# Last x rows loaded ahead, list rows of the last tiles scattered later, first expert's tokens and weights made ready ahead of a loop

## The chip, the cores and the metric

The kernel runs on one core of one Trainium2 chip. The metric is the device time of one execution in microseconds (us); the median of three executions is taken. Engines are named as in the profile: PE (TensorE matmuls) with PEld (its weight loads), DVE (VectorE), ACT (ScalarE), POOL (GpSimd), SP (SyncE). A q behind the name (SPq, POOLq) is the engine's sequencer, where DMA issues, branches and semaphore waits are recorded.

## What is computed

One decoder layer over 4096 tokens of width 1024: a normed and modulated input, a sliding-window attention beside a gated recurrence, an output projection, a residual, and then a mixture of 32 experts in 4 groups, of which each token takes two.

```python
h = rmsnorm(x, ln1_pre) * (1 + sc1) + sh1
attn, hg = ...                                # attention, recurrence
mix = concat([attn, hg]) @ w_out
x = x + ga1 * rmsnorm(mix, ln1_post)          # x rows are read again here
h = rmsnorm(x, ln2_pre) * (1 + sc2) + sh2
g = top1(softmax(h @ w_rg + b_rg))            # group of the token
e = top2(softmax(logits of that group))       # its two experts, weights normed
y = sum over the two: w_e * ((silu(h @ w_gate[e]) * (h @ w_up[e])) @ w_down[e])
x = x + ga2 * rmsnorm(y, ln2_post)
```

## The kernel before

The tokens are 32 tiles of 128 rows. Every float32 product is made of three products of split parts. Stage one (`sweep1`) makes the projections of the recurrence, stage two (`sweep2`) attention, output projection, residual, second norm and routing, stage three (`experts`) the experts. A planner (`Weave`) writes out the order: generators yield what they wait for, a model clock (`Clock`) holds a due time for each, and the instruction of whichever is due is recorded next. What results is one fixed order for each engine, and each engine runs its own in order.

Names for the end of stage two, tile n:

- `g_out(n)`: output projection into PSUM `ps_j`, two halves of 512 columns; ACT sums the squares and DVE multiplies by `mod0`, both into `ym`, shown as tile `x` (three buffers, so `ym` of tile 31 takes that of tile 28).
- `g_post(n)`: loads the x rows of the tile (`xt`, shown as `xr`, two buffers) by a DMA on SP; POOL makes the root (`ryv`, `ryr`); DVE makes the residual `x<-x,ryr,xr`; SP writes it to `out`. DVE or POOL makes `h2` in the same tile `xr`; its root is `r2v`, `r2r`. SP writes `h2` to `h_d`. Tiles up to 29 then turn `h2` with a DMA transpose on SP (`h2T<-x`), tiles 30 and 31 on PE (`ps_t<-ident,xr`). PE makes the logits (`ps_s<-wr,h2T`), DVE adds the bias (`s<-ps_s,rs,br`).
- `g_route(m)`: for a batch of tiles (m=6: tiles 24 to 27; m=7: 28 and 29; m=8: 30 and 31) some forty small DVE operations find the two experts, the place in each expert's queue, and add to the running counts `cum`. Then POOL issues three scatters for each tile, each behind a small memset: two rows of `tab_d` (token, row of y, weight; one for each expert) and one row of `list_d` (token number by its row in the group).
- `g_order`: between these, the experts in order of their size (`eord`), from the counts after tile 27.

Stage three. Expert r in that order is place r; it has room for a fixed number of tokens (`CAPS`, up to 384, so two or three tiles). SP loads the three matrices of place 0 (`ws`) as soon as `eord` is there. A loop whose count `n_over` is only known on the chip (lines 1986 and 1987) does what exceeds the room; here the count is zero, and it is jumped over. Behind it POOL gathers `trow`, the table rows of all places, PE turns them, DVE makes `tok` (token numbers), `yrow` and `wgt`; POOL gathers the token rows of place 0 (`xg<-h_d,tok`, four buffers). For each place PE turns the tokens (`ps_x`), ACT and DVE split them (`xT`), PE makes gate and up (`ps_g`), then down (`ps_d`); ACT and DVE split the weights (`w<-ws`, eight buffers). POOL scatters the results to `y_d`. `g_list` works out the rows of the list and reads the list back (`ti`), for the last step, which adds both results of a token, norms them and adds them to `out`.

Of the kernel before, what the change touches and what calls it, by code (L numbers as in the profile page):

```python
# [214 lines left out]
class Ring:  # L215
# [10 lines left out]
    def next(self):  # L226
        return self.slots[len(self.out) % self.bufs]
# [45 lines left out]
class Layer:  # L273
# [59 lines left out]
    def setup(self, ctx):  # L333
# [21 lines left out]
        self.pm = cst.tile([32, 32], F32, name="pm")  # L355
        self.cap = cst.tile([P, 32], BF, name="cap")
        self.trows = cst.tile([P, 1], I32, name="trows")
        self.spacer = cst.tile([1, 1], F32, name="spacer")

    def pools(self, ctx):  # L360
# [780 lines left out]
    def sweep2(self, w16a):  # L1141
# [7 lines left out]
        with ExitStack() as ctx:  # L1149
# [207 lines left out]
            def g_out(n):  # L1357
                while ("mT", n) not in st or (n >= 3 and ("h2T", n - 3) not in st):
                    yield WAIT
                mT = st["mT", n]  # L1360
                yield [mT]
                ym = xp.tile([P, D], F32, name="x", bufs=3)
                ss = sm.tile([P, 2], F32, name="ssy")
                for c in range(2):
                    pj = ps_j.tile([P, 512], F32, name="ps_j")
                    for k in range(KC):
                        while ("wo", k) not in st:
                            yield WAIT
                        for i, (u, v) in enumerate(((0, 0), (0, 1), (1, 0))):
                            nc.tensor.matmul(pj, mT[:, k, v], wo[:, k, u, c * 512:(c + 1) * 512],  # L1370
                                             start=(k == 0 and i == 0), stop=(k == KC - 1 and i == 2))
                        yield 0
                    yc = ym[:, c * 512:(c + 1) * 512]
                    nc.scalar.activation(yc, pj, AF.Square, scale=osc[:, 3:4], accum_out=ss[:, c:c + 1])
                    nc.vector.tensor_tensor(yc, pj, G1[:, c * 512:(c + 1) * 512], op=ALU.mult)
                st["y", n] = ym, ss
                wv.add(g_post(n))

            def g_post(n):
# [2 lines left out]
                while "fill" not in st:  # L1382
                    yield WAIT
                ym, ss = st["y", n]
                xt = op.tile([P, D], F32, name="xr")
                nc.sync.dma_start(xt, a["x"][0, n * P:(n + 1) * P, :])
                yield [ss, ym]
                r = self.rstd(sm, ss[:, 0:1], 1, D, "ry", also=ss[:, 1:2])
                yield
# [79 lines left out]
            def g_route(m):  # L1469
# [118 lines left out]
                yield  # L1588
                nc.vector.tensor_mul(pl[:, :, 1, 2], pl[:, :, 0, 2], gm[:, 3])
                nc.vector.tensor_add(cum, cum, cs)  # L1590
                if m == max(0, NT // RB - 2):
                    wv.add(g_order())
                st["routed", m] = True
# [3 lines left out]
                for b in range(B):  # L1597
                    for c in range(2):
                        self.scatter(self.tab_d, sl[:, c, b:b + 1], pl[:, b, c], "tab", "other rows of the table")
                        yield rest  # L1600
                    self.scatter(self.list_d, sl[:, 2, b:b + 1], idi[:, n0 + b:n0 + b + 1], "list",
                                 "other rows of the list")
                    yield rest
# [238 lines left out]
    def experts(self):  # L1842
# [5 lines left out]
        with ExitStack() as ctx:  # L1848
# [122 lines left out]
                return nc.sync.value_load(eord[0:1, r:r + 1], min_val=0, max_val=31)  # L1971

            order = ((0, 0), (1, 0), (0, 1), (1, 1), (2, 0), (2, 1))
            places = [(r, i, f) for r in range(32) for i, f in order]


            st, lows = {}, []
# [3 lines left out]
            rp = ent(tc.tile_pool(name="r_p", bufs=1, reuse_waits="tile"))  # L1981
            steps = self.order(cp, rp, ps_x)
            next(steps)


            n_over = nc.values_load(self.nover[0:1, 0:1], min_val=0, max_val=P)
            with tc.For_i(0, n_over, 1) as it:
# [36 lines left out]
                    out=self.y_d, out_offset=bass.IndirectOffsetOnAxis(ap=oi[:, 2:3], axis=0), in_=y,  # L2024
                    in_offset=None, bounds_check=2 * T - 1, oob_is_err=False)
                for ring in (W, XG, XT, Y, YY):
                    ring.gone.update(ring.out)


            for _ in range(2):  # L2030
                next(steps)
            for j in range(tile_n[0]):
                load_x(0, j, run(XG.take()))
            run(steps)

            eord = cp.tile([P, 32], I32, name="eord")
            nc.gpsimd.tensor_copy(eord, self.eord)
# [124 lines left out]

            def g_list():

                yield 12000.0
                yield from self.list_rows(cp, fp)
                yield
                y = yield from Y.take()
# [114 lines left out]
```

## Time and profile before

| | us |
|---|---|
| median of three executions | 2732.44 (2731.12 to 2740.7) |
| profiled execution, its own time | 2765.53 |
| span of the profile | 2763.8 |
| PE busy in the span | 2510.2 (91%) |
| DVE busy | 1905.7 (69%) |
| ACT busy | 1360.1 (49%) |
| POOL busy | 756.7 (27%) |

The page's row of busy tenths for PE is 9 nearly throughout, with a hole at about two thirds of the span, where stage two ends and stage three begins, and another in the last 50 us. The granted clock is full elsewhere, with short falls, and half in these two holes.

### The profile page before, as it was taken

To read this page: it belongs to the slowest core of one execution; us is meant where nothing else is said; L and a number is where in the kernel's file an instruction comes from. 1 tells how busy PE (TensorE), PEld (TensorE's weight loads), DVE (VectorE), ACT (ScalarE), POOL (GpSimd) and SP (SyncE) were. 2 spreads that over 40 slices of the span, in tenths; PEclk is the share of its full clock that TensorE was granted. 3 is DMA by queue.
4 is the path that set the end of the run, shared out by engine and by line. 5 is a ranking of instruction groups with operands and counts; after the bars stand their busy time and mean duration, and the time that the engine had idled before them with its cause. 6 is when DMAs were issued, how large, how long until landed. Compare 5 with 4: busy or idle time off the path is not lost. (4 is left out here: it accounts for less than half of the span.)

```text
span 2763.8 us, 50275 instructions
## 1 busy us (share of the span) xinstructions
PE 2510.2 (91%) x19433; PEld 1916.5 (69%) x19433; DVE 1905.7 (69%) x4109; ACT 1360.1 (49%) x2935; POOL 756.7 (27%) x1069
## 2 busy tenths in 40 slices
PE   5989999999999999989999999955999999999992
PEld 2767677677667676666666676624888888889981
DVE  5657657777776688878778778664555666566774
ACT  4435444334333355555555545523545656666662
POOL 0111212211211012132232331343442333233336
PEclk9999999999999999999999999977999999999996
DMA  8212222222222334343453453445655878788987
GB/s 278 88 62 77 96 72 73 83 91 75 70 88 83 109 119 126 119 93 97 117 117 93 108 115 94 77 129 187 215 174 188 295 258 270 280 274 286 324 284 215
DMA packets 194619, 414.46 MB, mean 150 GB/s; under 512 B 89069, under 2 KB 124057, under 8 KB 172873
## 3 DMA queue, kind: packets, MB, share of 16 engines
q1 hardware_dynamic: 157216, 319.06, 36.6%
q0 software_dynamic: 31584, 91.58, 11.3%
q8 instruction: 153, 2.51, 0.4%
q10 hardware_dynamic: 5576, 0.58, 0.2%
q14 instruction: 90, 0.73, 0.1%
HBM read 284.60 MB, written 118.16 MB: 146 GB/s over the span
## 5 line engine op out<-in xcount | busy, mean ns | idle before, releaser
L140 PE MATMUL ps_g<-xT,w 128*128 128x256 f32 (+8 forms) x3072 | 461.5, 305 | 0.0
L140 PEld LDWEIGHTS ps_g<-xT,w 128*128 128x128 f32 x3072 | 436.2, 189 | 7.1 <-issue 0.3
L140 PE MATMUL ps_j<-w,mT 128*128 128x512 f16 x1536 | 368.2, 384 | 0.0
L140 PE MATMUL ps_j<-hT,w 128*128 128x256 f16 x3072 | 349.0, 274 | 4.9 <-POOL hT L140 4.9
L140 PE MATMUL ps_j<-w,hT 128*128 128x512 f16 x1536 | 349.7, 380 | 0.0
L140 PEld LDWEIGHTS <-w 128*128 128x128 f16 x3072 | 301.9, 98 | 47.1 <-issue 8.4
L140 PEld LDWEIGHTS <-hT 128*128 128x128 f16 x2304 | 196.6, 99 | 167.2 <-issue 6.7
L140 PE MATMUL ps_d<-w,av 128*128 128x512 f32 (+6 forms) x1020 | 269.1, 407 | 3.9 <-ACT av L140 3.5
L140 ACT ACTIVATE w<-ws 128x512 fp32r<-128x512 f32 (+1 forms) x392 | 246.1, 678 | 32.5 <-issue 23.5
L140 DVE TENSOR_TENSOR w<-ws,w 128x512 fp32r<-128x512 f32 x384 | 245.3, 685 | 5.4 <-ACT w L140 5.3
L140 PEld LDWEIGHTS <-mT 128*128 128x128 f16 x1536 | 144.3, 99 | 148.4 <-issue 12.3
L140 DVE TENSOR_TENSOR xT<-ps_x,xT 128x256 fp32r<-128x256 f32 (+8 forms) x256 | 115.5, 472 | 170.3 <-ACT xT L140 160.2
L140 PE MATMUL ps_j<-hT,w16a 128*128 128x256 f16 x1920 | 222.4, 275 | 0.0
L140 PEld LDWEIGHTS ps_d<-w,av 128*128 128x128 f32 (+6 forms) x1020 | 177.6, 182 | 51.6 <-ACT av L140 5.2
L140 PEld LDWEIGHTS <-w16a 128*128 128x128 f16 x1920 | 188.1, 99 | 25.7 <-issue 0.6
L140 POOL TENSOR_TENSOR hT<-hf,hT 128x512 f16<-128x512 f32 x64 | 103.6, 1619 | 270.0 <-ACT hT L140 255.2
L140 ACT ACTIVATE y<-ps_d,wgt 128x512 f32<-128x512 f32 (+4 forms) x144 | 99.0, 688 | 121.2 <-PE ps_d L140 88.5
L140 PE MATMUL ps_x<-ident,xg 128*128 128x128 f32 (+7 forms) x680 | 127.4, 294 | 28.5 <-DMA xg<-h_d,tok 23.9
L140 ACT ACTIVATE s<-s,mx,qsc 128x256 f32<-128x256 f32 (+1 forms) x256 | 148.8, 584 | 0.0
L140 PEld LDWEIGHTS ps_x<-ident,xg 128*128 128x128 f32 (+7 forms) x680 | 106.3, 193 | 56.5 <-DMA xg<-h_d,tok 28.3
L140 ACT ACTIVATE xT<-ps_x 128x256 fp32r<-128x256 f32 (+8 forms) x256 | 101.3, 422 | 88.5 <-PE ps_x L140 80.2
L140 POOL DMA_INDIRECT y_d<-y,yrow x85 | 91.1, 1072 | 193.3 <-ACT y L140 153.9
(397 smaller groups left out, 4242.3 us busy)
## 6 DMA issues: line engine op xcount, KB each, us to landing
ws<-in_w_exp_gate_dram SPq DMA_DIRECT2D x32, 1024.0 KB
ws<-in_w_exp_up_dram SPq DMA_DIRECT2D x32, 1024.0 KB
ws<-in_w_exp_down_dram SPq DMA_DIRECT2D x32, 1024.0 KB
yy<-y_d SPq DMA_DIRECT2D x24, 1024.0 KB
x<-in_x_dram SPq DMA_DIRECT2D x32, 512.0 KB
hT_d<-hT SPq DMA_DIRECT2D x16, 1024.0 KB
m_w<-in_w_ada_dram SPq DMA_DIRECT2D x128, 128.0 KB
hT<-hT_d SPq DMA_DIRECT2D x16, 1024.0 KB
```

What stands on the lines that cost most here:

```text
L140: r = f(*a, **kw)
```

## The change

Three things. (1) At tile 30's output projection the x rows of tiles 30 and 31 are loaded into one buffer that held a block of stage one's `hT` (shown as tile `hT`), and `g_post` of these two tiles uses it instead of `xr`; no load is issued there. (2) The list rows of tiles 24 to 31 are not scattered by `g_route`; DVE keeps a copy of their places (`lsl`), and `g_list` scatters the eight columns in stage three, 3000 ns of planner's time apart, ahead of its other work. (3) Ahead of the loop over `n_over` stand now the gather of `trow`, its transposes, `tok`, the gathers of place 0's tokens, and the split of its gate and up weights. The loop's own buffers are counted so that what is held stays held.

```diff
--- before.py
+++ after.py
@@ -355,6 +355,7 @@
         self.pm = cst.tile([32, 32], F32, name="pm")
         self.cap = cst.tile([P, 32], BF, name="cap")
         self.trows = cst.tile([P, 1], I32, name="trows")
+        self.lsl = cst.tile([P, 8], I32, name="lsl")
         self.spacer = cst.tile([1, 1], F32, name="spacer")
 
     def pools(self, ctx):
@@ -1358,6 +1359,12 @@
                 while ("mT", n) not in st or (n >= 3 and ("h2T", n - 3) not in st):
                     yield WAIT
                 mT = st["mT", n]
+                if n >= NT - 2:
+                    if n == NT - 2:
+                        st["lx"] = Cut(hp.tile([P, KC, 2, NB], F16, name="hT", bufs=2))
+                        for i in (n, n + 1):
+                            st["lx", i] = st["lx"].tile([P, D], F32)
+                            nc.sync.dma_start(st["lx", i], a["x"][0, i * P:(i + 1) * P, :])
                 yield [mT]
                 ym = xp.tile([P, D], F32, name="x", bufs=3)
                 ss = sm.tile([P, 2], F32, name="ssy")
@@ -1382,8 +1389,11 @@
                 while "fill" not in st:
                     yield WAIT
                 ym, ss = st["y", n]
-                xt = op.tile([P, D], F32, name="xr")
-                nc.sync.dma_start(xt, a["x"][0, n * P:(n + 1) * P, :])
+                if n >= NT - 2:
+                    xt = st["lx", n]
+                else:
+                    xt = op.tile([P, D], F32, name="xr")
+                    nc.sync.dma_start(xt, a["x"][0, n * P:(n + 1) * P, :])
                 yield [ss, ym]
                 r = self.rstd(sm, ss[:, 0:1], 1, D, "ry", also=ss[:, 1:2])
                 yield
@@ -1588,6 +1598,9 @@
                 yield
                 nc.vector.tensor_mul(pl[:, :, 1, 2], pl[:, :, 0, 2], gm[:, 3])
                 nc.vector.tensor_add(cum, cum, cs)
+                if n0 >= NT - 8:
+
+                    nc.vector.tensor_copy(self.lsl[:, n0 - NT + 8:n0 - NT + 8 + B], sl[:, 2])
                 if m == max(0, NT // RB - 2):
                     wv.add(g_order())
                 st["routed", m] = True
@@ -1598,6 +1611,8 @@
                     for c in range(2):
                         self.scatter(self.tab_d, sl[:, c, b:b + 1], pl[:, b, c], "tab", "other rows of the table")
                         yield rest
+                    if n0 >= NT - 8:
+                        continue
                     self.scatter(self.list_d, sl[:, 2, b:b + 1], idi[:, n0 + b:n0 + b + 1], "list",
                                  "other rows of the list")
                     yield rest
@@ -1971,7 +1986,7 @@
                 return nc.sync.value_load(eord[0:1, r:r + 1], min_val=0, max_val=31)
 
             order = ((0, 0), (1, 0), (0, 1), (1, 1), (2, 0), (2, 1))
-            places = [(r, i, f) for r in range(32) for i, f in order]
+            places = [(r, i, f) for r in range(32) for i, f in order][4:]
 
 
             st, lows = {}, []
@@ -1981,6 +1996,29 @@
             rp = ent(tc.tile_pool(name="r_p", bufs=1, reuse_waits="tile"))
             steps = self.order(cp, rp, ps_x)
             next(steps)
+            next(steps)
+
+            def first_weights(fs):
+
+                for i, f in fs:
+                    ws = st["ws", 0, i]
+                    w = run(W.take())
+                    t, part = pieces(w, ws, i, f)
+                    for p in part:
+                        nc.scalar.activation(p[0], p[2], AF.Copy)
+                        low(*p)
+                    st["w", 0, i, f] = t, w
+                    if f:
+                        WS.drop(ws)
+
+
+            first_weights(order[:2])
+            next(steps)
+            for j in range(tile_n[0]):
+                load_x(0, j, run(XG.take()))
+            run(steps)
+            first_weights(order[2:4])
+            held = {R: len(R.out) for R in (W, XG, XT, Y, YY)}
 
 
             n_over = nc.values_load(self.nover[0:1, 0:1], min_val=0, max_val=P)
@@ -2024,14 +2062,8 @@
                     out=self.y_d, out_offset=bass.IndirectOffsetOnAxis(ap=oi[:, 2:3], axis=0), in_=y,
                     in_offset=None, bounds_check=2 * T - 1, oob_is_err=False)
                 for ring in (W, XG, XT, Y, YY):
-                    ring.gone.update(ring.out)
-
-
-            for _ in range(2):
-                next(steps)
-            for j in range(tile_n[0]):
-                load_x(0, j, run(XG.take()))
-            run(steps)
+                    ring.gone.update(ring.out[held[ring]:])
+
 
             eord = cp.tile([P, 32], I32, name="eord")
             nc.gpsimd.tensor_copy(eord, self.eord)
@@ -2162,7 +2194,13 @@
 
             def g_list():
 
-                yield 12000.0
+                yield 6000.0
+                tl = fp.tile([P, 8], I32, name="tl")
+                nc.gpsimd.iota(tl, pattern=[[P, 8]], base=T - 8 * P, channel_multiplier=1)
+                for n in range(8):
+                    self.scatter(self.list_d, self.lsl[:, n:n + 1], tl[:, n:n + 1], "list",
+                                 "other rows of the list")
+                    yield 3000.0
                 yield from self.list_rows(cp, fp)
                 yield
                 y = yield from Y.take()
```

What the change does to the order, at three places. First SP, from the x load of tile 29 to the weights of place 0. Before:

```order
L140 DMA xr<-in_x_dram 128x1024
L140 DMA h_d<-xr 128x1024
L140 DMA out_dram<-x 128x1024
L140 DMA h_d<-xr 128x1024
L140 DMA_TRANSPOSE h2T<-x 128x16x128
L140 DMA xr<-in_x_dram 128x1024
L140 DMA out_dram<-x 128x1024
L140 DMA h_d<-xr 128x1024
L140 DMA_TRANSPOSE h2T<-x 128x16x128
L140 DMA xr<-in_x_dram 128x1024
```

And now:

```order
L140 DMA xr<-in_x_dram 128x1024
L140 DMA hT<-in_x_dram 128x1024 x2
L140 DMA h_d<-xr 128x1024
L140 DMA out_dram<-x 128x1024
L140 DMA h_d<-xr 128x1024
L140 DMA_TRANSPOSE h2T<-x 128x16x128
L140 DMA out_dram<-x 128x1024
L140 DMA h_d<-hT 128x1024
L140 DMA_TRANSPOSE h2T<-x 128x16x128
L140 DMA out_dram<-x 128x1024
```

The loads of tiles 30 and 31 stood behind the transposes of tiles 28 and 29; now both stand right behind the load of tile 29.

Second DVE, from the residual of tile 30 on (`pl_22235` and `pl_22239` are batch m=6's entries for the table, `mod` with a number the modulation rows). Before:

```order
L140 SCALAR_TENSOR_TENSOR x<-x,ryr,xr 128x1024
L140 RECIPROCAL gm<-gm 128x4
L140 TENSOR_TENSOR x<-ps_j,mod_10465 128x512
L140 SCALAR_TENSOR_TENSOR s<-ps_s,rs,br 128x36
L140 SCALAR_TENSOR_TENSOR s<-ps_s,rs,s 128x36
L140 TENSOR_TENSOR pl_22235<-gm 128x4
L140 TENSOR_TENSOR xr<-x,mod_10466 128x1024
L140 TENSOR_TENSOR x<-ps_j,mod_10465 128x512
L140 TENSOR_TENSOR pl_22235<-pl_22235,gm 128x4
L140 TENSOR_TENSOR cum<-cum,cs 128x36
L140 SCALAR_TENSOR_TENSOR xr<-xr,r2r,mod_10467 128x1024
```

And now:

```order
L140 SCALAR_TENSOR_TENSOR x<-x,ryr,hT 128x1024
L140 RECIPROCAL gm<-gm 128x4
L140 TENSOR_TENSOR pl_22239<-gm 128x4
L140 TENSOR_TENSOR pl_22239<-pl_22239,gm 128x4
L140 TENSOR_TENSOR cum<-cum,cs 128x36
L140 COPY lsl<-sl 128x4
L140 TENSOR_TENSOR hT<-x,mod_10467 128x1024
L140 TENSOR_TENSOR x<-ps_j,mod_10466 128x512
L140 SCALAR_TENSOR_TENSOR hT<-hT,r2r,mod_10468 128x1024
L140 SCALAR_TENSOR_TENSOR s<-ps_s,rs,br 128x36
L140 SCALAR_TENSOR_TENSOR s<-ps_s,rs,s 128x36
L140 SCALAR_TENSOR_TENSOR x<-xr,rs,x 128x1024
```

Batch m=6's last three operations moved up to right behind the residual of tile 30, and the split of tile 29 (last row, ahead of its DMA transpose) follows the logits of tile 28.

Third POOL, from the last scatters of the routing over the loop (lines 1986 and 1987 before, 2024 and 2025 now) to the first gathers behind it; the loop's body is left out by taking two pieces. Before, the last scatters and, behind the loop, the first gathers:

```order
L140 DMA tab_d<-s 131072x3
L140 MEMSET spacer 1x1
L140 DMA tab_d<-s 131072x3
L140 MEMSET spacer 1x1
L140 DMA list_d<-idi,s 16384x1
L1986 TENSOR_LOAD nover
L1987 COMPARE_AND_BRANCH
```

```order
L1987 UNCONDITIONAL_BRANCH
L140 DMA trow<-tab_d,trows 128x384
L140 DMA xg<-h_d,tok 128x1024 x3
L140 COPY eord<-eord 128x32
L140 DMA xg<-h_d,tok 128x1024
```

And now, the last scatters and what stands ahead of the loop, then behind it:

```order
L140 DMA tab_d<-s 131072x3
L140 MEMSET spacer 1x1
L140 DMA tab_d<-s 131072x3
L140 DMA trow<-tab_d,trows 128x384
L140 DMA xg<-h_d,tok 128x1024 x3
L2024 TENSOR_LOAD nover
L2025 COMPARE_AND_BRANCH
```

```order
L2025 UNCONDITIONAL_BRANCH
L140 COPY eord<-eord 128x32
L140 IOTA tl 128x8
L140 MEMSET spacer 1x1
L140 DMA list_d<-tl,lsl 16384x1
L140 DMA xg<-h_d,tok 128x1024 x4
L140 MEMSET spacer 1x1
L140 DMA list_d<-tl,lsl 16384x1
L140 MEMSET spacer 1x1
L140 DMA list_d<-tl,lsl 16384x1
```

The gathers moved from behind the loop to ahead of it, and list scatters stand behind it, among the gathers of place 1.

## Rows read from the trace of the kernel before

**Rows 1.** Windows by stage: span, then busy us (instructions) by engine, PEclk, DMA share, GB/s.

```profile
1820.00:1860.00 40.00, 13.01 (x108) 8.90 (x107) 23.35 (x117) 7.00 (x15) 17.98 (x31) 0.61 0.50 102
1860.00:1900.00 40.00, 4.18 (x16) 2.42 (x15) 13.37 (x63) 7.78 (x15) 18.22 (x30) 0.50 0.43 151
1900.00:2707.00 807.00, 783.25 (x4751) 702.75 (x4752) 503.01 (x912) 478.92 (x946) 285.25 (x385) 0.98 0.75 260
```

**Rows 2.** Waits of PE, 1815 to 1905: waiter, waited for, total, times, longest.

```profile
PE ps_x L140 <- DMA trow<-tab_d,trows: 24.0, 1, 24.0
```

**Rows 3.** Timeline, SP and DVE at tiles 29 to 31: start, duration, engine, operation, [idle before].

```profile
1818.81 1.11 SPq L140 DMA_DIRECT2D xr<-in_x_dram  x1
...
1823.34 1.28 DVE L140 SCALAR_TENSOR_TENSOR x<-x,ryr,xr 128x1024 f32<-128x1024 f32 x1 [6.10 <-DMA xr<-in_x_dram]
...
1830.29 1.88 SPq L140 DMA_TRANSPOSE h2T<-x  x1
...
1832.23 1.00 SPq L140 DMA_DIRECT2D xr<-in_x_dram  x1
...
1840.85 1.28 DVE L140 SCALAR_TENSOR_TENSOR x<-x,ryr,xr 128x1024 f32<-128x1024 f32 x1 [10.56 <-POOL spacer L140]
```

**Rows 4.** Timeline, what else tile 31's residual needs: ACT, PE, POOL.

```profile
1821.32 0.69 ACT L140 ACTIVATE x<-ps_j,qsc 128x512 f32<-128x512 f32 x1 [7.04 <-DMA h2T<-x]
...
1821.76 2.75 PE L140 MATMUL ps_j<-w,mT 128*128 128x512 f16 x12
...
1830.39 0.57 POOL L140 TENSOR_TENSOR ryr<-ryv,mhalf 128x1 f32<-128x1 f32 x1
```

**Rows 5.** Timeline, logits of tiles 29 and 31 and the counts after m=7, m=8.

```profile
1835.73 0.90 PE L140 MATMUL ps_s<-wr,h2T 128*128 128x72 f16 x16 [7.77 <-DMA h2T<-x]
...
1848.24 1.94 PE L140 MATMUL ps_t<-ident,xr 128*128 128x128 f32 x8 [3.80 <-DVE s L140]
...
1852.27 0.26 DVE L140 SCALAR_TENSOR_TENSOR s<-ps_s,rs,br 128x36 f32<-128x36 f32 x1 [0.39 <-PE ps_s L140]
...
1860.13 0.17 DVE L140 TENSOR_TENSOR cum<-cum,s 128x36 bf16<-128x36 bf16 x1
...
1863.25 0.17 DVE L140 TENSOR_TENSOR cum<-cum,s 128x36 bf16<-128x36 bf16 x1
```

**Rows 6.** Timeline of POOL, first and last of twelve scatters, then behind the loop.

```profile
1860.31 1.06 POOL L140 DMA_INDIRECT tab_d<-s  x1 [13.48 <-DVE cum L140]
...
1874.30 0.96 POOL L140 DMA_INDIRECT list_d<-idi,s  x1 [0.22 <-POOLq L1987]
1885.13 0.99 POOL L140 DMA_INDIRECT trow<-tab_d,trows  x1 [9.87 <-issue]
```

**Rows 7.** Line 1987, 1880.0 to 1881.5: operation, count, ns min/median/max, first and last start.

```profile
L1987 POOLq INC_SWDGE_SEM  x1: 2092/2092/2092, 1880.9 to 1880.9; - x1
```

**Rows 8.** Timeline behind the loop, to the first product of place 0.

```profile
1884.76 6.59 ACT L140 ACTIVATE w<-ws 128x512 fp32r<-128x512 f32 x12 [23.52 <-issue]
...
1890.20 0.95 POOL L140 DMA_INDIRECT xg<-h_d,tok  x1 [4.08 <-DVE yrow L140]
...
1898.29 1.11 PE L140 MATMUL ps_x<-ident,xg 128*128 128x128 f32 x4 [1.09 <-DMA xg<-h_d,tok]
...
1900.49 1.31 PE L140 MATMUL ps_g<-xT,w 128*128 128x384 f32 x3
```

**Rows 9.** Timeline of PE in stage three, waits for tokens (places 3, 6 and 8).

```profile
1962.89 1.06 PE L140 MATMUL ps_x<-ident,xg 112*128 112x112 f32 x4 [3.99 <-DMA xg<-h_d,tok]
...
2054.46 1.29 PE L140 MATMUL ps_x<-ident,xg 64*128 64x64 f32 x4 [3.00 <-DMA xg<-h_d,tok]
2118.40 0.79 PE L140 MATMUL ps_x<-ident,xg 128*128 128x128 f32 x4 [3.55 <-DMA xg<-h_d,tok]
```

**Rows 10.** Windows of PE alone: span, busy us (instructions), PEclk, DMA share, GB/s.

```profile
2040.00:2070.00 30.00, 27.00 (x127) 0.83 0.54 184
2070.00:2100.00 30.00, 30.00 (x168) 1.00 0.54 184
```

## The prediction

> **What bounds the kernel now.** I read the busy tenths first, then windows by stage. PE works nearly without a break except where stage two ends: of the 80 us from 1820 to 1900 it works 17 [rows 1]. From 1900 to 2707 it is busy 97% of the time, so what moves the first product of place 0 moves the end by as much, unless stage three itself changes. The waits of PE say which wait ends last in the hole: 24.0 us for the gathered table rows `trow` [rows 2]. From there I went back by the timeline. `trow` is issued by POOL at 1885.13, after the loop and after twelve scatters that began at 1860.31, when DVE had the counts of batch m=7 [rows 5, 6]. These wait for the logits of tiles 29 to 31, and these for two DVE operations, the residuals of tiles 30 and 31, before which DVE stood 6.1 and 10.6 us [rows 3]. The second wait is put down to a POOL memset that was long done; the x load issued at 1832.23 is what was outstanding, and its partner, issued at 1818.81, took until 1823.34 [rows 3]. So the chain through the hole is: x row, residual, logits, routing, scatters, loop, table, tokens, first product at 1900.49 [rows 8].
>
> **Part 1, x rows ahead.** Removed: two loads that stood on SP behind the DMA transposes of tiles 28 and 29. They now run behind the load of tile 29, beside PE work of two tiles; I cost them at nothing, and if that cover were gone it would be one load, 4.5 us (1818.81 to 1823.34) [rows 3]. No new wait: the buffer's block was read long before. What is late next, step by step:
> The residual of tile 30 starts 6.1 us earlier, at 1817.2. Behind it on DVE now comes the end of batch m=6, then the first half of tile 31's projection, which cannot start before ACT's at 1821.32: ACT waits there for the transpose of tile 28, whose buffer tile 31 takes [rows 4]. So DVE has h2 of tile 30 at about 1824, then logits of tile 28 (0.5) and the split of tile 29 (1.3), and the transpose of tile 29 is issued at 1825.8 instead of 1830.29. It took 5.44 us before (1830.29 to 1835.73) [rows 3, 5]; I keep that: 1831.2.
> The residual of tile 31 needs PE's last twelve products, which end at 1824.5 [rows 4], then ACT, 0.9, and POOL, 0.9: 1826.7 instead of 1840.85. Even with `ryr` at 1830.96 as before [rows 4] it would be 9.9 us earlier; I take 14.1. Its h2 reaches PE 7.4 us later as before (1840.85 to 1848.24) [rows 3, 5], at 1834.1.
> The logits of tile 29 stand before it on PE: 1831.2 plus 0.9, then tile 30's transposes (1.9) and ACT, DVE and the logits behind the second half of them (0.7 to 0.9 each), 1836.2. That is later than 1834.1 and decides. From tile 31's transposes to DVE's logits it took 4.03 us (1848.24 to 1852.27), from there to the two counts 7.86 and 10.98 us [rows 5]. So the count of m=7 stands at 1848.1 instead of 1860.13: **12.0 us earlier**. The bounds: 8 (the routing operations of DVE, some 18 us of work from tile 29's logits on, close up less) and 14.
>
> **Part 2, list rows later.** Removed from the chain: list scatters at 1.27 us each ((1874.30 - 1860.31) / 11) [rows 6]. Eight leave stage two, but four of them lay in batch m=6, beside DVE's waits, and count nothing. Behind the count of m=7 there were twelve scatters; now there are ten, not eight, because in POOL's new order two of m=6's stand behind the first of m=7. So the last begins 9 x 1.27 = 11.4 us after the first instead of 14.0: **2.5 us**. With the first at 1848.3, the last begins at 1859.7 instead of 1874.30. Added: three DVE copies of four columns at most (0.17 each, as the counts) [rows 5], and in stage three eight memset and scatter pairs, 10 us of POOL, which is busy 35% there [rows 1]. On POOL's queue the token gathers of places 1 to 3 stand behind them; who waits for those is PE. That is the third rival.
>
> **Part 3, place 0 ahead of the loop.** Before, the last scatter's start to `trow` took 10.83 us (1874.30 to 1885.13) [rows 6]. In it lie the landing of the scatters, until the sequencer's step at 1880.9 [rows 7], and from there the way through the loop, 3.9 us to ACT's first work at 1884.76 [rows 7, 8]. Then 5.07 to the first token gather, 8.1 until the third tile is at PE (1898.29) and 2.2 to the first product [rows 6, 8]: 26.2 in all. Now the same pieces stand in another order. The gather of `trow` waits for the landing alone. Its price: at least a gather's own 3.5 us, at most 7.9, from the last table scatter (1.27 before 1874.30) to 1880.9; I take 7, nearer to the end that measures scatters [rows 6, 7]. Then 5.07, then 8.1 until the tokens have landed, for which the loop now waits, 3.9 for the loop, and 3.2 for transposes and split, of which one us lay under the landing before: 27.3. So this part is **a wash, 1.1 us worse**, between 3 better and 2 worse. The split of eight weight pieces, 8 x 0.55 = 4.4 us of ACT (6.59 for twelve) [rows 8] and about as much of DVE, moves from behind the loop to where both engines idle for more than 20 us; it was off the path before too, since PE waited for tokens. If it were exposed it would cost 5.
>
> What stands first after the last scatter is thus 1859.7 + 27.3 = 1887.0 for the first product, against 1900.49: **13.5 us**.
>
> The Trainium skill (DMA: Bandwidth & Descriptors, Anatomy of one DMA, the GpSimd path) puts the fixed cost of one such DMA at about 2.0 us. The rows show 6.6 us from the last scatter's start to the step behind its landing [rows 6, 7], so the trace does not agree. By the rule alone, with before left as measured, the landing term would be 2 and this start 18.5 us earlier.
>
> **Stage three.** PE waits for tokens at places 3, 6 and 8 for 4.0, 3.0 and 3.55 us [rows 9], and each wait has a stretch at half clock behind it: 127 products in the 30 us around place 6's, 168 in the next 30 [rows 10]. The planner now puts the transposes of places 4 to 8 later among the products of the place before. I counted in both orders the products between the last transpose of one place and the first of the next, the time in which the tokens land, and gave them their share of the stage's 783 us of work [rows 1]: it goes from 5.5 to 7.7 us up to 11 to 17. That should remove the waits of places 6 and 8 (6.5 us, and up to as much again at half clock). For places 2 and 3 it falls slightly (6.4 to 6.1 and 5.6), and list rows land there. I take 5 us gained, between 12 gained and 5 lost.
>
> **Sum.** 13.5 + 5 = 18.5 us. The profiled execution's own time is 2765.53, 33.1 above the median; I carry the difference over as it is: 2732.44 - 18.5 = 2713.9, so 2714.
>
> **Rivals.**
> First, the routing binds and not the x rows. If tile 29's transpose lands hardly earlier than at 1835.7, or DVE's list does not close up, the count of m=7 moves by 8 only, and stage three keeps its waits: 8 + 2.5 - 1.1 gives 2723.0. For it: DVE was busy 23 of the 40 us of the hole's first half [rows 1]. Against: two waits of 16.7 us stand in the middle of it.
> Second, the change does not do what it says: the residuals wait for something else as long as for the loads, and the gather of `trow` takes the loop's wait. Gain 2 to 5, 2729. Against: the list of part 1 finds nothing that late.
> Third, slower: list rows hold up the token gathers. One wait as at place 3 costs 4.0, and about as much at half clock [rows 9, 10], 8 together. Two of them eat the gain of 13.5; from four on it is slower beyond the bound below. Five, at places 1 to 5, give 2732.4 - 13.5 + 40 = 2759. For it: place 3's wait fell where POOL mixed small gathers and token gathers. Against: place 1's tokens have 16 us, and POOL has idle time for the rows.
> The Trainium skill (DMA: Bandwidth & Descriptors, Queues, rings and completion order) says that a DMA's count is raised only after every earlier write of that DMA engine, across its queues; by that rule the token gathers would wait for the list rows' writes, as in the third rival. The x load of tile 31, 8.6 us among scatters against 4.5 for tile 30's [rows 3], agrees with it.
> Fourth, all token waits after place 2 go: 13.5 + 14, twice the waits' 7, gives 2705.
>
> **How the numbers follow.** Forecast 2714 (own range 2706 to 2719): 0.52. Fourth, better: 0.08. First: 0.26. Second: 0.07. Third: 0.07. A measurement of this kernel can tell about 0.5% from no change, 13.7 us: faster means below 2718.8. So faster 0.60, same 0.33, slower 0.07. The range 2703 to 2729 leaves out the slower cases, part of the second, and the far end of the fourth.
>
> **What would show it.** Right: no DVE wait before the residuals of tiles 30 and 31; the count of m=7 within 12 us of tile 31's logits; ten scatters behind it; about 27 us from the last scatter to the first product; no PE wait over 2 us at places 6 and 8. Wrong: a scatter-to-`trow` wait over 9 us, tokens landing more than 9 us after their issue ahead of the loop, or new PE waits for `xg` or `w` in places 1 to 5.

## The result

The change is faster: 2720.6 us in the median of seven executions (2713.6 to 2725.1) against 2736.0 (2731.1 to 2740.7), 15.4 us less; ratio 0.9935, 95% interval 0.992 to 0.995. Timed again beside its parts the ratio was 0.9921 (0.9906 to 0.9936). That is more than the 0.5% that a measurement of this kernel tells from no change, on the forecast's side, and inside the range 2703 to 2729; the prediction's own narrower range, 2706 to 2719, missed it by 1.6 us.

One thing has to be known for all that follows: the level differs between chips. The kernel before took 2763, 2746, 2744 and 2738 us in the median on the four chips of the experiments. The profiled execution shown ahead (2765.53) lies at the level of the slowest of them, so two spans can't be subtracted. Times are compared on one chip only, and places in two traces are counted from one event ahead of the change's reach: the issue of the DMA transpose of tile 28, 1816.95 in [rows 3].

The chain of the prediction, in the timeline of the changed kernel (start, duration, engine, operation; in brackets the idle time before it and what ended it):

```profile
1794.35 1.32 SPq L140 DMA_TRANSPOSE h2T<-x  x1
1794.55 1.27 DVE L140 SCALAR_TENSOR_TENSOR x<-x,ryr,hT 128x1024 f32<-128x1024 f32 x1
...
1803.33 1.88 SPq L140 DMA_TRANSPOSE h2T<-x  x1
1804.04 1.28 DVE L140 SCALAR_TENSOR_TENSOR x<-x,ryr,hT 128x1024 f32<-128x1024 f32 x1
...
1823.82 0.17 DVE L140 TENSOR_TENSOR cum<-cum,s 128x36 bf16<-128x36 bf16 x1
1823.99 0.96 POOL L140 DMA_INDIRECT tab_d<-s  x1 [10.43 <-DVE s L140]
...
1835.52 0.96 POOL L140 DMA_INDIRECT tab_d<-s  x1 [0.22 <-issue]
1838.66 0.99 POOL L140 DMA_INDIRECT trow<-tab_d,trows  x1 [2.18 <-DMA tab_d<-s]
1843.34 0.95 POOL L140 DMA_INDIRECT xg<-h_d,tok  x1 [3.69 <-DVE tok L140]
...
1852.71 1.54 PE L140 MATMUL ps_x<-ident,xg 128*128 128x128 f32 x6 [9.97 <-POOL spacer L140]
...
1855.34 1.31 PE L140 MATMUL ps_g<-xT,w 128*128 128x384 f32 x3
```

The residuals of tiles 30 and 31 (the first two DVE rows) wait for no load any more: no bracket. Behind the count of m=7 (`cum`) POOL issues ten scatters without a gap; `trow` now names its own wait, the landing of the scatters, 2.18 us. Counted from the DMA transpose of tile 28:

| | before [rows 3 to 8] | after | predicted shift | measured shift |
|---|---|---|---|---|
| residual of tile 30 | 6.4 | 0.2 | -6.1 | -6.2 |
| residual of tile 31 | 23.9 | 9.7 | -14.1 | -14.2 |
| count of m=7 | 43.2 | 29.5 | -12.0 | -13.7 |
| last scatter | 57.4 | 41.2 | -14.6 | -16.2 |
| first product of place 0 | 83.5 | 61.0 | -13.5 | -22.6 |
| end of the span | 946.8 | 917.4 | -18.5 | -29.4 |

The hole by windows, as in [rows 1] (busy us of each engine and instructions, then PE's granted clock, DMA share and GB/s):

```profile
1790.00:1820.00 30.00, 20.05 (x144) 12.11 (x141) 24.70 (x102) 8.31 (x18) 11.29 (x25) 0.76 0.41 122
1820.00:1860.00 40.00, 9.12 (x48) 7.54 (x49) 18.78 (x107) 8.29 (x17) 16.71 (x28) 0.54 0.51 174
1860.00:1900.00 40.00, 36.02 (x196) 33.32 (x196) 18.72 (x37) 21.17 (x42) 17.20 (x27) 0.96 0.90 206
```

This execution is 23 us ahead when it comes to the hole, so the first window already holds part of it, and these windows can't be set against those of [rows 1] one by one. From the DMA transpose of tile 28 to the first product PE works 20.2 of 61.0 us, where it worked 20.7 of 83.5 before: the same work with 22 us less of waiting. The granted clock is near half (0.54 of full) in the middle window alone.

PE's waits for tokens in stage three, timeline:

```profile
1891.94 0.38 PE L140 MATMUL ps_x<-ident,xg 128*128 128x128 f32 x1 [2.94 <-DMA xg<-h_d,tok]
...
2135.93 1.06 PE L140 MATMUL ps_x<-ident,xg 48*128 48x48 f32 x4 [3.31 <-DMA xg<-h_d,tok]
...
2173.84 0.45 PE L140 MATMUL ps_x<-ident,xg 128*128 128x128 f32 x1 [3.57 <-DMA xg<-h_d,tok]
```

The waits of places 3, 6 and 8 [rows 9] are gone; there are new ones at place 2, where list rows stand ahead of the tokens, and at places 11 and 12 (the tiles of 48 rows). All waits for tokens behind place 0 come to 18.7 us, 16.2 before. From the first product to the end it takes 856.4 us, 863.3 before.

So the start moved 9 us further than predicted, and the end of the two traces moved 29 us where the times moved 15. The experiments had to say which part gave what.

### The profile page after: what moved, and what is told of

It reads as the page before. It is cut to its first block, busy times and chain, and to the rows that moved or that the text cites. A ratio compares the mean times of both kernels' runs of the same rounds, so it can differ in the third digit from the quotient of the medians.

```text
span 2711.8 us, 50265 instructions
## 1 busy us (share of the span) xinstructions
PE 2492.6 (92%) x19433; PEld 1908.7 (70%) x19433; DVE 1907.8 (70%) x4115; ACT 1359.8 (50%) x2932; POOL 753.3 (28%) x1070
## 3 DMA queue, kind: packets, MB, share of 16 engines
q0 software_dynamic: 31584, 91.58, 11.7%
## 5 line engine op out<-in xcount | busy, mean ns | idle before, releaser
L140 PE MATMUL ps_d<-w,av 128*128 128x512 f32 (+6 forms) x1020 | 261.8, 402 | 4.7 <-ACT av L140 4.4
L140 PE MATMUL ps_x<-ident,xg 128*128 128x128 f32 (+7 forms) x680 | 123.5, 289 | 29.4 <-DMA xg<-h_d,tok 18.7
L140 POOL DMA_INDIRECT xg<-h_d,tok x85 | 87.4, 1028 | 204.8 <-PE ps_x L140 184.6
```

The source lines that it names most:

```text
L140: r = f(*a, **kw)
```

## The experiments

All are counted as above. "Stage three" is from the first product to the end of the span; the ratio is to the kernel before on the same chip.

| kernel | ratio (95%) | count m=7 | last scatter | first product | stage three |
|---|---|---|---|---|---|
| before, as shown | | 43.2 | 57.4 | 83.5 | 863.3 |
| before_again | 0.9999 (0.9986 to 1.0012) | 43.1 | 57.3 | 84.4 | 856.1 |
| x_rows_alone | 0.9977 (0.9964 to 0.9990) | 29.2 | 53.6 | 79.0 | 860.4 |
| list_later_alone | 1.0015 (1.0002 to 1.0027) | 40.2 | 49.3 | 72.4 | 869.5 |
| place0_alone | 0.9996 (0.9984 to 1.0008) | 43.6 | 58.2 | 81.7 | 865.3 |
| x_rows_and_list | 0.9991 (0.9980 to 1.0003) | 29.4 | 40.9 | 64.1 | 876.3 |
| x_rows_and_place0 | 0.9989 (0.9977 to 1.0002) | 30.3 | 55.4 | 81.6 | 861.9 |
| list_and_place0 | 0.9961 (0.9945 to 0.9976) | 40.9 | 50.5 | 72.2 | 852.4 |
| all_three | 0.9921 (0.9906 to 0.9936) | 29.4 | 41.7 | 61.5 | 856.1 |
| list_spread | 1.0013 (1.0004 to 1.0023) | 29.5 | 41.4 | 61.6 | 882.6 |
| list_spread_no_place0 | 1.0014 (1.0000 to 1.0027) | 29.4 | 41.0 | 62.8 | 876.7 |
| list_bunch | 0.9971 (0.9961 to 0.9981) | 29.4 | 41.2 | 61.1 | 870.9 |
| list_after_place1 | 0.9930 (0.9917 to 0.9944) | 29.4 | 40.9 | 61.5 | 861.8 |

### Each part alone

Part 1 alone:

```diff
+                if n >= NT - 2:
+                    if n == NT - 2:
...
+                            nc.sync.dma_start(st["lx", i], a["x"][0, i * P:(i + 1) * P, :])
```

> Before with part 1 alone: the x rows of tiles 30 and 31 are loaded ahead, nothing else. The order of PE in stage three is word for word that of before. By the prediction the residuals of tiles 30 and 31 start 6 and 14 us earlier, measured from the DMA transpose of tile 28, the count of m=7 12 to 14 us earlier, and the time falls by 12 (2720), with the token waits of places 3, 6 and 8 still there. If the routing binds (first rival): 8 less at the most. If the gain of the whole change lies in its other parts: 5 less or nothing.

Part 2 alone (`lsl`, no list scatter for the last tiles in `g_route`, eight in `g_list`):

```diff
+                    if n0 >= NT - 8:
+                        continue
...
-                yield 12000.0
+                yield 6000.0
```

> Before with part 2 alone: the eight list scatters of the last tiles stand in stage three. By the prediction 2.5 us less from two scatters fewer behind the count of m=7, and nothing lost in stage three: 2 to 3 faster, hardly to be told from no change. If list rows hold token gathers (third rival): a PE wait of 3 to 4 us for tokens among the places where they land, and 1 to 6 us slower.

Part 3 alone (`trow`, tokens and `first_weights` ahead of the loop):

```diff
-            places = [(r, i, f) for r in range(32) for i, f in order]
+            places = [(r, i, f) for r in range(32) for i, f in order][4:]
...
+            first_weights(order[:2])
+            next(steps)
```

> Before with part 3 alone: place 0's tokens and weights ahead of the loop. This part alone also reorders stage three, since the planner starts with place 0's weights done. By the prediction the start is a wash, 1 us worse, and the reordering gives 5: 4 us faster. If the scatters land in 2 to 3 us whatever stands around them, and the loop's exit costs 1.2 us and not 3.9: the start gains 2 to 6, and with the reordering 7 to 11 faster. If the reordering is worth nothing: between 1 slower and 2 faster.

And the whole change beside them, with no edit:

> The whole change again, beside its parts on one chip: 15 us faster, as measured. If the parts add up, the three runs beside it sum to this; if they share a cover (one part's gain hides another's), the sum is larger.

The parts don't add up: by the ratios 6.3 less, 4.1 more and 1.1 less, 3.3 less together, but 21.8 less as a whole. The whole gained more than the expected 15, and its parts sum to less than it, which neither branch of that expectation had. The list rows alone came out as their rival said (1 to 6 slower), place 0 alone as the branch in which the reordering is worth nothing. With the x rows alone the count of m=7 came 14 us earlier, as predicted, but the last scatter by 3.8 only. The timeline of that kernel shows why:

```profile
1840.49 0.17 DVE L140 TENSOR_TENSOR cum<-cum,s 128x36 bf16<-128x36 bf16 x1
1840.65 0.98 POOL L140 DMA_INDIRECT tab_d<-s  x1 [9.90 <-DVE s L140]
...
1853.47 0.96 POOL L140 DMA_INDIRECT list_d<-idi,sl  x1 [1.65 <-DMA tab_d<-s]
...
1864.83 0.95 POOL L140 DMA_INDIRECT list_d<-idi,s  x1 [0.22 <-issue]
1874.19 0.99 POOL L140 DMA_INDIRECT trow<-tab_d,trows  x1 [8.40 <-issue]
```

Nineteen scatters stand behind the count, against twelve before, and they end with POOL, not DVE, as what is late: 24.2 us from the first to the last at 1.27 each, with one stop of 1.65. Before, the other seven had gone out while DVE waited for the x rows. POOL's scatters were a second chain of nearly the same length, and the prediction had priced part 1 as if part 2 were there.

The list rows alone move the last scatter by 8 us and the first product by 11 to 12, and the kernel is no faster: stage three takes 869.5. PE stands 13.8 us there for the tokens of place 1, which POOL issued behind all eight list scatters:

```profile
1915.69 0.45 PE L140 MATMUL ps_x<-ident,xg 128*128 128x128 f32 x1 [8.88 <-DMA xg<-h_d,tok]
1919.37 0.48 PE L140 MATMUL ps_x<-ident,xg 128*128 128x128 f32 x1 [3.23 <-DMA xg<-h_d,tok]
1921.55 1.12 PE L140 MATMUL ps_x<-ident,xg 128*128 128x128 f32 x4 [1.71 <-DMA xg<-h_d,tok]
```

### Pairs, and the kernel before once more

```diff
 # x_rows_and_list: parts 1 and 2
 # x_rows_and_place0: parts 1 and 3
 # list_and_place0: parts 2 and 3
 # before_again: no edit
```

> The change without part 3: x rows ahead and list rows later, place 0 as before behind the loop. Theory now: early x rows alone make POOL's scatters the bound (last scatter 53.6 us after the DMA transpose of tile 28, against 57.4 before), list rows later alone leave DVE's waits; only together they move the last scatter to 41 or 42. Then the first product, by before's way through the loop, at 65 to 67 (61.6 with all three, 83.6 before), and stage three stays as with the list rows alone, 865 to 870: 10 to 15 faster than before. Rival: the parts add as measured alone, 7.6 less and 1.9 more: 6 faster, the last scatter at 46 to 50.

> The change without part 2: the list rows stay among the scatters of stage two. Theory now: POOL's scatters bind, the last one at 53 to 54 us after the DMA transpose of tile 28, about 19 scatters behind the count of m=7, the first product at 73 to 77, stage three 860 to 865: 6 to 10 faster. If the list rows in stage two cost only the two scatters of the prediction (2.5): 17 faster or more, last scatter at 44 to 45.

> The change without part 1: the x loads stay behind the DMA transposes. Theory now: DVE's waits for the x rows stay, the count of m=7 at 40 to 43 us after the DMA transpose of tile 28, last scatter at 49 to 50, first product at 69 to 73 instead of 61.6: 8 to 11 slower than the whole change, 10 to 13 faster than before. If the x rows are worth no more than alone: within 8 of the whole change. By the prediction's 12 us: 12 slower than the whole.

> The kernel before on this chip, for its trace. The whole change's trace shows 29 us less from the DMA transpose of tile 28 to the end than the trace shown of before, the times 15 to 23. If the trace shown of before is a typical one, this one has again some 947 us from there to the end, 10 to 11 us from the last scatter to the table gather, and the same token waits. If it was an unlucky one: 938 to 942, with scatters that land in 2 to 4 us.

The last scatter came within 1.5 us of what the theory said, in all three: 41, 55 and 50.5. The pair without part 2 stays with before (0.9989, expected 6 to 10 us faster): POOL binds, and the first product comes at 81.6 instead of 73 to 77. The pair without part 1 is 7 to 11 us short of the whole, about what it starts later (72.2 against 61.5).

But the pair without part 3 missed: its first product comes 20 us ahead of before's, and nothing of it arrives. Its stage three is 20 us longer than that of before_again. PE in that kernel, from the first product to place 1:

```profile
1867.97 1.31 PE L140 MATMUL ps_g<-xT,w 128*128 128x384 f32 x3
...
1873.23 10.39 PE L140 MATMUL ps_g<-xT,w 128*128 128x384 f32 x57
1894.41 0.45 PE L140 MATMUL ps_x<-ident,xg 128*128 128x128 f32 x1 [10.79 <-DMA xg<-h_d,tok]
1898.11 0.48 PE L140 MATMUL ps_x<-ident,xg 128*128 128x128 f32 x1 [3.25 <-DMA xg<-h_d,tok]
1900.12 1.12 PE L140 MATMUL ps_x<-ident,xg 128*128 128x128 f32 x4 [1.53 <-DMA xg<-h_d,tok]
```

PE makes 75 of place 0's 96 gate and up products and then stands 15.6 us for the tokens of place 1. POOL's DMAs of 1855 to 1885 (tiles, engine, count, median us from issue to landing, of the two in each group whose landing this view gives):

```profile
list_d<-tl,lsl POOLq DMA_INDIRECT x8, 17.0
xg<-h_d,tok POOLq DMA_INDIRECT x7, 19.3
```

The eight list scatters were put ahead of place 1's tokens. By the times of the semaphores in the trace (a DMA has landed when its semaphore has its full count) seven of them took 16 to 19 us to land, and the tokens behind them 18 to 24. That is the prediction's third rival, at about twice the 8 us that it gave one wait. In the whole change place 1's tokens stand behind one of them.

The second trace of before has the same start as the first (84.4 against 83.5), the long way from the last scatter to `trow` too (11.8 against 10.8); its stage three is 7 us shorter. So neither branch of that expectation came whole: the start is a property of the order, and stage three differs by 7 us between two executions of the same kernel. Against this trace the end moved by 23 us, not 29.

### Where the list rows stand

Theory now: a list scatter holds up the tokens issued behind it. Rival: part 3 itself makes stage three short. First the list rows late, one or two at a time, with and without part 3, and late in a bunch (in the bunch with 80000 and 3000):

```diff
-                yield 6000.0
+                yield 100000.0
...
-                    yield 3000.0
+                    yield 12000.0
```

> The whole change, but the eight list scatters of stage three come one or two at a time between the token gathers of places 6 to 10, instead of among those of places 1 to 3. If list rows among token gathers are what holds PE at places 1 and 2 (third rival): those PE waits, 4 us, go, and 3 to 8 us less than the whole change, 20 to 27 less than before. If the start of stage three is held by the weight loads and not by list rows: the same waits, within 3 us of the whole change.

> As x_rows_and_list (place 0 as before, behind the loop), with the list scatters one or two at a time between the token gathers of places 5 to 9. There the first product came 20 us earlier, and PE then stood 15.6 us for the tokens of place 1, which were issued behind eight list scatters. If the list scatters are the cause: the wait falls under 3 us, stage three takes 856 to 862 us instead of 876, and the time is 12 to 20 below before, within 8 of the whole change. If it is place 0's early weights that make stage three short: the wait stays over 10 us, and the time stays within 5 of before.

> The whole change, but the eight list scatters stand in a bunch among the token gathers of place 5, with four of them right before them. If a bunch of list scatters holds the next tokens wherever it stands: those gathers take 12 to 20 us, a PE wait of 3 us or more at place 5 or 6, and about the time of the whole change. If it only hurts where place 1's and 2's weights come in at the same time: no such wait, and as fast as with the list rows spread.

The times fell out against both theories: 3.6 and 3.8 us slower than before, and the bunch 8.0 faster. The traces say why. Without part 3 the wait at place 1 did go, from 15.6 to 1.2 us, and up to the thirteenth of 32 equal parts of stage three's gate and up products both spread kernels were still 21 and 24 us ahead of before_again. Then they lost 17 and 16 us over the next eight. Late list rows make the reading back of the list late, and the planner puts the transposes of places 11 to 14 close together: those of place 13 stand within 7.8 us with next to no products between them, in the changed kernel within 20.3 us with 14.3 us of products. PE in list_spread, a little further on (places 14 and 15):

```profile
2261.16 0.82 PE L140 MATMUL ps_x<-ident,xg 128*128 128x128 f32 x4 [0.66 <-DVE xT L140]
2262.64 0.83 PE L140 MATMUL ps_x<-ident,xg 128*128 128x128 f32 x4 [0.66 <-DVE xT L140]
2264.12 1.11 PE L140 MATMUL ps_x<-ident,xg 128*128 128x128 f32 x4 [0.65 <-DVE xT L140]
...
2267.96 9.57 PE L140 MATMUL ps_g<-xT,w 128*128 128x256 f32 x55 [1.10 <-DVE w L140]
```

Transpose upon transpose, each waiting for DVE to clear the last, and the granted clock was 0.90 between 2250 and 2300. PE also waited for tokens at places 6, 8, 9 and 10, between which the list rows now stand (3.65, 4.33, 1.27 and 2.65 us; none over 0.7 there in the whole change), and the last step ended 4.7 us later behind PE's last product (57.4 against 52.7). These losses were foreseen by neither theory; how much each of them costs I did not take apart.

The bunch shows the hold by itself, at place 5, far from place 1's and 2's weights:

```profile
1983.26 0.48 PE L140 MATMUL ps_x<-ident,xg 128*128 128x128 f32 x1 [6.86 <-DMA xg<-h_d,tok]
...
1987.12 1.01 PE L140 MATMUL ps_x<-ident,xg 96*128 96x96 f32 x4 [3.38 <-DMA xg<-h_d,tok]
```

Those tokens, issued behind the list and y scatters, took 15 to 17.5 us; the three issued ahead of them at 1940 took 5 to 6.4.

The last kernel sets the two theories apart without the late order: parts 1 and 2 alone, with the list rows only 10 us of planner's time later, behind place 1's tokens:

```diff
-                yield 6000.0
+                yield 16000.0
```

> Parts 1 and 2 without part 3, as x_rows_and_list, with the first list scatter of stage three 10 us later: the eight then stand behind the token gathers of place 1, among those of places 2 and 3, about where the whole change has them. Theory now: part 3 gives 1 to 2 us at the start, the rest of what it does is to move place 1's tokens ahead of the list scatters. Then the first product comes 62 to 64 us after the DMA transpose of tile 28, PE does not stand for tokens at place 1, and from the transpose to the end it is 915 to 922 us, 14 to 22 faster than before. Rival: part 3 is needed for stage three (its order with place 0's weights done): 932 or more, within 8 of before. With list_spread a second thing was seen that may also act here: the order of places 9 to 14 changes when list and table work comes later; it would show there as PE waits and not at places 1 to 3.

It is as fast as the whole change: 0.9930 (0.9917 to 0.9944), 2717.0 us against 2738.0; from the transpose to the end 923 us (917 with the whole change, 940 in before_again). Its timeline:

```profile
1824.28 0.17 DVE L140 TENSOR_TENSOR cum<-cum,s 128x36 bf16<-128x36 bf16 x1
...
1835.80 0.96 POOL L140 DMA_INDIRECT tab_d<-s  x1 [0.22 <-POOLq L2002]
1841.27 0.99 POOL L140 DMA_INDIRECT trow<-tab_d,trows  x1 [4.51 <-issue]
...
1856.36 1.31 PE L140 MATMUL ps_g<-xT,w 128*128 128x384 f32 x3
...
1874.06 0.71 PE L140 MATMUL ps_x<-ident,xg 128*128 128x128 f32 x4 [0.85 <-DMA xg<-h_d,tok]
...
1891.00 0.43 PE L140 MATMUL ps_x<-ident,xg 128*128 128x128 f32 x1 [2.75 <-DMA xg<-h_d,tok]
1893.81 1.12 PE L140 MATMUL ps_x<-ident,xg 128*128 128x128 f32 x4 [2.37 <-DMA xg<-h_d,tok]
```

Place 0 goes by before's way, behind the loop, and its first product comes 61.5 us after the transpose of tile 28, as with part 3 (61.0 and 61.5). Place 1's tokens cost 0.85 us; place 2's, of which two of three tiles now stand behind four list scatters, cost 5.1 (the last two rows). So part 3 isn't needed at the start, and what it did for the whole was to put place 1's tokens ahead of seven of the eight list scatters. No kernel here beat the whole change by more than the intervals.

## Why the prediction was right, and where its steps were not

**What bounds.** Right: the hole is one chain, and the end follows the first product where no token wait stands behind it. Where one does (x_rows_and_list), 20 us of start arrive as nothing.

**Part 1.** The residuals to 0.1 us; the count 13.7 us earlier, predicted 12.0 (bounds 8 to 14). The transpose of tile 29 took 4.4 us, not 5.44. The first rival (routing binds) fell. But the step is right only with part 2: the prediction did not ask what POOL's queue would do with an earlier count, and alone part 1 moves the last scatter by 3.8.

**Part 2.** Ten scatters behind the count: right; the last begins 11.7 us after the count instead of 14.2, 2.5 us. As a price of part 2 this was far too small, since without it POOL binds: 0.9977 and 0.9989 with the x rows in and the list rows unmoved.

**Part 3.** "A wash" is right: 61.5 without it (list_after_place1), 61.0 to 61.5 with it; over all pairs of kernels beside the same other parts it is between 3.1 better (x_rows_and_list 64.1) and 2.6 worse (x_rows_alone 79.0, x_rows_and_place0 81.6). Its terms were not right. From the last scatter to the first product it was 26.2 us before, was to be 27.3, and is 19.8: the landing 3.1 instead of 7, the gathers until all tokens are there about as said (4.7 and 8), the loop 1.5 instead of 3.9. The landing is the term that was mis-sized most, and what shortens it is part 2 with part 1, not part 3. By the times of the semaphores in the traces the last scatter landed 6.9 and 7.8 us after its issue in the two traces of before and 6.3 after it in place0_alone; 4.7 in list_later_alone and 4.5 in list_and_place0; and 2.1 (list_after_place1) to 3.7 (list_spread_no_place0) where parts 1 and 2 are both in, 2.3 in the changed kernel. The 7 was measured among list scatters; with part 3 alone, which leaves them there, it is what was predicted:

```profile
1870.37 0.95 POOL L140 DMA_INDIRECT list_d<-idi,s  x1 [0.22 <-issue]
1877.24 0.99 POOL L140 DMA_INDIRECT trow<-tab_d,trows  x1 [5.91 <-DMA tab_d<-s]
```

That is 6.9 us. The list rows are not all of it: the way from the last scatter to `trow` is 5.9 without part 2, 5.3 without part 1, 3.1 and 3.4 with both. What part 1 does to it no run takes apart. Part 3 itself lets `trow` go 0.8 us after the last table row has landed, where before's way through the loop took 1.8 to 4.0, and pays 1.5 for the loop behind the tokens.

The Trainium skill (DMA: Bandwidth & Descriptors, Anatomy of one DMA, the GpSimd path) puts the fixed cost of such a DMA at about 2.0 us. The prediction set this aside against the row of before; the changed kernel's last scatter, 2.3 us to its landing and 3.1 to `trow`, is nearer to it than to the 7. A start 18.5 us earlier, which the prediction gave by that rule, was nearer to the measured 22.6 than its own 13.5.

**Stage three.** Predicted 5 gained. The waits named did go, but others came (18.7 and 12.4 us of waits for tokens behind place 0 in two traces of the whole change, 16.2 and 19.6 in two of before), and stage three took 856.4 and 856.1 us against 863.3 and 856.1 in two traces of before: between 7 and nothing. It is not a gain of the change that could be told from the scatter of one kernel's executions.

**Third rival.** It was given 0.07 as an outcome. As a mechanism it is real: 15.6 us in x_rows_and_list, 13.8 in list_later_alone, both at place 1. How much of it is left in the whole change is not shown. Its two traces wait 3.9 us (2.94 and 0.94) and 0.7 us for the tokens of place 2; the prediction had named new token waits in places 1 to 5 as a sign of being wrong. But PE waits more there in place0_alone, which has none of the eight list rows in stage three:

```profile
1932.88 0.48 PE L140 MATMUL ps_x<-ident,xg 128*128 128x128 f32 x1 [2.26 <-DMA xg<-h_d,tok]
1936.62 1.12 PE L140 MATMUL ps_x<-ident,xg 128*128 128x128 f32 x4 [3.27 <-DMA xg<-h_d,tok]
```

In x_rows_and_place0, which has none either, it is 6.7 us. In both, those tokens stand behind a y scatter and another scatter into the list (`list_d<-none,last`), so the wait at place 2 can't be put down to the rows that were moved.

The Trainium skill (DMA: Bandwidth & Descriptors, Queues, rings and completion order) says that a DMA's count rises only after the earlier writes of that DMA engine. The traces agree: tokens landed 9 to 24 us after their issue behind list scatters (18 to 24 behind all eight) and 4 to 10 with none ahead of them. What kept the wait small in the change is where the planner happened to put the list rows.

**The sum.** 18.5 predicted, 15.4 by the medians, 17.8 and 21.8 by the two ratios. It came out because a start that was 9 us too small and a stage three that was up to 5 too large partly cancelled; that is luck, not a merit of the sum. The rest, 23 us in traces of the two kernels beside a time of 15 to 22, is within what single executions scatter: on one chip those of before run from 2737 to 2756.

## What to carry to other kernels

Before a wait is priced, look at what else is queued on the next engine of the chain: removing DVE's wait left POOL's scatters as the bound, so that it paid only together with the edit that thinned them out. A duration taken from a burst (a landing of 7 us) belongs to what stands in the burst, so when the change takes things out of it, the duration must be taken from a quieter row. And where small transfers are moved out of a critical stretch, check which transfer follows them on that queue: the gain of 20 us at the start was lost whole to the next place's tokens, a position 10 us of planner's time later gave most of it back, and one far later lost it again to the order that the planner made around it.

## What was not expected of the hardware

A scatter of 128 list numbers is short for POOL (0.96 us) but takes long to land, and more so in a row: the first of the eight in x_rows_and_list took 6.7 us, the other seven 15.7 to 19.1; one or two at a time, in list_spread, they took 4.7 to 12.4. The last table scatter in list_after_place1 took 2.1. While the eight were under way little else came through. Busy tenths of the 16 DMA engines and GB/s in x_rows_and_list, 1855 to 1885 in 40 slices:

```profile
DMA  0006798999899994076999979209797959941239
GB/s 0 0 0 98 284 366 279 350 371 312 279 371 142 153 55 33 0 218 262 415 449 306 99 77 44 22 11 99 66 77 77 66 77 120 131 22 11 22 121 377
```

From 1871.5 to 1881.3 the engines show as busy for most of the time, but move 11 to 131 GB/s, weights included. The changed kernel moved 48 and 66 GB/s in the two stretches of 4 us from 1872 to 1880, list_bunch 33 to 53 in three from 1964 to 1976, each right behind list scatters. So the tokens did not wait because the weights took the bandwidth.

The landing was long also where the DMA engines had next to nothing to do. The same two rows in before_again, 1850 to 1875:

```profile
DMA  9999920400000000000000000000000000017978
GB/s 406 421 407 446 396 71 13 29 0 1 0 2 0 1 0 3 0 3 0 1 0 0 0 0 0 0 0 0 0 0 0 0 0 0 13 13 190 367 232 303
```

From about 1855 on the engines stand near zero. The table scatters issued from 1855.47 to 1859.26, with list scatters among them, landed from 1866.7 to 1868.1, and `trow`, behind them and the loop, was issued at 1872.29. The last bytes before `trow` went in the slice at 1862, so the wait is not one for bandwidth: it lies between the bytes and the count. A table scatter inherits it: each of the sixteen steps by which the semaphore of the one issued at 1855.47 rose came 0.16 to 0.21 us behind a step of the list scatter issued ahead of it, at 1854.21. Why the list scatter's own count comes so late no run here shows.
